# The gate of layer 0's attention sub-layer: its matrix-vector product moved from VectorE to column groups of TensorE

## The chip, the cores and the metric

The kernel runs on one core of a Trainium2 chip. The metric is device microseconds of one execution, lower is better. TensorE appears in the profile as PE (matmuls) and PEld (weight loads), VectorE as DVE, ScalarE as ACT, GpSimd as POOL, and the queue that issues the transfers as SP.

## What is computed

Two layers of an encoder trunk on 256 tokens of width 2048. In each layer a conditioning vector `c` gives six vectors of 2048 numbers (shift, scale and gate, for the attention sub-layer and for the feed-forward one). Each of the six is a product of a vector with a 2048 x 2048 matrix.

```python
cond = jax.nn.silu(c)
for l in range(DEPTH):
    mod = cond @ w_ada[l] + b_ada[l]
    sh1, sc1, g1, sh2, sc2, g2 = [m[:, None, :] for m in jnp.split(mod, 6, axis=-1)]
    u = x * (1.0 + sc1) + sh1
    proj = u @ w_in[l]
    ...
    y = jnp.concatenate([rms_norm(ya, ...), rms_norm(yb, ...), rms_norm(yc, ...)], axis=-1)
    x = layer_norm(DEEPNORM_ALPHA * x + (1.0 + g1) * (y @ w_o[l]), ln1_g[l], ln1_b[l])
    u = x * (1.0 + sc2) + sh2
    gu = u @ w_gu[l]
    h = jax.nn.silu(gu[..., :D_FF]) * gu[..., D_FF:]
    x = layer_norm(DEEPNORM_ALPHA * x + (1.0 + g2) * (h @ w_down[l]), ln2_g[l], ln2_b[l])
```

`ya`, `yb` and `yc` are three groups of attention heads (4, 6 and 6 heads) on slices of `proj`. The change is about `g1` of layer 0, which is needed for the first time at the output projection `y @ w_o[0]`.

## The kernel before

All data lie transposed: features on the 128 partitions, tokens along the free axis. Every weight matrix streams from HBM once, as pieces of 128 x 2048 fp32 (1 MB), through four buffers with the tag `raw` (`RAWB = 4`). For the large products a piece is split into two parts, `hi` (ACT, rounded) and `lo` (DVE, the rest), and TensorE multiplies these in its fast fp32r form; in layer 0 three matmuls of 256 columns stand for each 128 x 128 block (L289 to L291). Attention scores, the transposition of the probabilities (`ptp`), the product with V (`y`) and the small statistics (`st`) are plain fp32 matmuls.

The six modulation vectors are called parts 0 to 5: 0 and 1 are shift and scale of the attention, 2 is its gate, 4 and 3 scale and shift of the feed-forward, 5 its gate. Each part is 16 pieces of `w_ada`, which pass through the same four `raw` buffers. A piece holds, on its partitions, 128 outputs with all 2048 inputs along the free axis. One DVE instruction (L205, `tensor_tensor_reduce`) multiplies the piece with `cond`, copied to all partitions, and sums along the free axis to one column of `mods[l, part]`; a second tiny one writes the sum out. So there are 192 such instructions in the kernel.

They are dealt out in a fixed order by `pace`, which takes so many pieces off the list `ada_pending` per weight load or attention head; `need` takes what is left before a part is used. Parts 0 and 1 of layer 0 come at the very start, then the 16 pieces of part 2, then parts 4 and 3. Part 2's pieces run beside the stretch in which layer 0's input projection ends, group a's heads run, the latent projections (`in_22`, `in_20`, `in_21`, `in_16` to `in_19`, then `kn`, `vb`, `qn`, `qp`) are made, and group b's heads begin. A list scheduler orders the instructions on each engine by priority and readiness; pieces of part 2 have priority -1000, which puts them behind other work that is ready. On the chip each engine then goes through its list strictly in that order.

PSUM accumulators for the projections come from four banks of tag `g`; the transposed probabilities `pt` of the heads lie in two SBUF buffers of tag `pts`.

Of the kernel before, what the change touches and what calls it, by code (L numbers as in the profile page):

```python
# [10 lines left out]
F32 = mybir.dt.float32  # L11
F32R = mybir.dt.float32r
AF = mybir.ActivationFunctionType
ALU = mybir.AluOpType
# [3 lines left out]
P = 128  # L18
D = 2048
S = 256  # L20
L = 2
KT = D // P
# [11 lines left out]
ALPHA = (2 * L) ** 0.25  # L34
# [52 lines left out]
T2K, T1K, RAWB, HIB = 28, 24, 4, 4  # L87
# [2 lines left out]
RATE = ((0.19, 0.135, 0.135), (0.04, 0.05, 0.05))  # L90
NPOOL = 4


V_ADA, V_LN1G, V_LN1B, V_LN2G, V_LN2B = 0, 96, 112, 128, 144
V_QN, V_KVN, V_GN = 160, 164, 166

C_ID, C_FOLD, C_CS, C_MASK, C_ONES, C_DIST = 0, 128, 256, 512, 576, 704
NCONST = 1088
SLOPES = [float(np.float32(2.0 ** (-8.0 * (i + 1) / C_HEADS))) for i in range(C_HEADS)]


@with_exitstack
def tile_encoder(ctx: ExitStack, tc: tile.TileContext, xT, cB, w_ada, vecs, rpb, sink, consts,
                 w_in, w_va, w_vc, w_uq, w_ukv, w_o, w_gu, w_dn, out):
    nc = tc.nc
    pe, ve, ac, po, sy = nc.tensor, nc.vector, nc.scalar, nc.gpsimd, nc.sync

    cst = ctx.enter_context(tc.tile_pool(name="cst", bufs=1))
    wp = ctx.enter_context(tc.tile_pool(name="wp", bufs=1))
    sb = ctx.enter_context(tc.tile_pool(name="sb", bufs=1))  # L110
# [24 lines left out]
    cs = cst.tile([P, NCONST], F32, name="cs")  # L135
# [3 lines left out]
    maskc = cs[:, C_MASK:C_MASK + GRID_W]  # L139
    ones = cs[:, C_ONES:C_ONES + P]  # L140
    dist = cs[:, C_DIST:C_DIST + 384]
    cond = cst.tile([P, D], F32, name="cond")
    crow = wp.tile([P, D], F32, tag="raw", bufs=RAWB, name="crow")
    sy.dma_start(out=crow[:1], in_=cB)
    vec = cst.tile([P, L * NVEC], F32, name="vec")
    sy.dma_start(out=vec, in_=vecs)
    snk = cst.tile([P, L * C_HEADS], F32, name="snk")
    nsnk = cst.tile([P, L * C_HEADS], F32, name="nsnk")

# [7 lines left out]
    for i in range(0, D, 512):  # L157
        cb = pg(f"cond{i}")
        pe.matmul(cb[:], lhsT=one[:1, :P], rhs=crow[:1, i:i + 512], start=True, stop=True)
        ac.activation(out=cond[:, i:i + 512], in_=cb[:], func=AF.Silu)  # L160
    xspin = cst.tile([P, 512], F32R, name="xspin")
    ac.activation(out=xspin, in_=cond[:, :512], func=AF.Copy)
    eps_ln = cst.tile([P, 1], F32, name="eps_ln")
# [10 lines left out]
    mods = {}  # L174
# [14 lines left out]
    def ada_finish(l, part, c0, n):  # L189

        m = mods[l, part][:, c0:c0 + n]
        if part in (2, 5):
            ve.tensor_scalar(out=m, in0=m, scalar1=1.0, scalar2=1.0 / ALPHA, op0=ALU.add, op1=ALU.mult)
        elif part in (1, 4):
            ac.activation(out=m, in_=m, func=AF.Copy, bias=1.0)

    def ada(n):
        for _ in range(n):
            if not ada_pending:
                return  # L200
            l, part, k = ada_pending.pop(0)
            w = wp.tile([P, D], F32, tag="raw", bufs=RAWB, name=f"ada{l}_{part}_{k}")
            sy.dma_start(out=w, in_=w_ada[l, part * KT + k])
            with after(gate[0]), tc.high_priority(100 if l == 0 and part < 2 else -1000):
                ve.tensor_tensor_reduce(out=w, in0=w, in1=cond, op0=ALU.mult, op1=ALU.add, scale=1.0,  # L205
                                        scalar=vcol(l, V_ADA + part * KT + k), accum_out=mods[l, part][:, k:k + 1])
            g = ada_group(l, part)
            if k % g == g - 1:
                ada_finish(l, part, k + 1 - g, g)

    credit = [0.0, 0.0]

# [386 lines left out]
    for l in range(L):  # L599
# [103 lines left out]
        for h in range(A_HEADS):  # L703
            nv = nba[:, h].rearrange("p (r c) -> p r c", c=GRID_W)
            ve.scalar_tensor_tensor(out=nv, in0=nv, scalar=-1.0,
                                    in1=maskc.unsqueeze(1).to_broadcast([P, 6, GRID_W]),
                                    op0=ALU.mult, op1=ALU.add)
# [44 lines left out]
        for h in range(B_HEADS):  # L752
            acc = pg(f"kn{l}_{h}")
# [6 lines left out]
        for h in range(2):  # L760
            for j in range(2):
                acc = pg(f"vb{l}_{h}_{j}")
# [10 lines left out]
        for g in range(3):  # L773
            get = wload(w_uq[l, g], 2048, (1024, 1024))
            for j in range(2):
                h = 2 * g + j
                acc = pg(f"qn{l}_{h}")
# [3 lines left out]
                acc = pg(f"qp{l}_{h}")  # L781
# [35 lines left out]
        for n in range(KT):  # L817
# [5 lines left out]
            acc = pg(f"o{l}_{n}")  # L823
# [33 lines left out]
        for g in range(FFG):  # L857
            credit[1] = RATE[l][1 if g == 0 else 2]
            H = []
            for j in range(GSZ):  # L860
                f = g * GSZ + j
                hs = []
                for w in range(2):
# [5 lines left out]
                    if 2 * f + w < HB and l:  # L869
                        acc = head[2 * f + w]  # L870
                    else:
                        get = wload(w_gu[l, 2 * f + w], 2048, (1024, 1024))
                        acc = pg(f"gu{l}_{f}_{w}")
# [11 lines left out]
                if g == FFG - 1:  # L885
                    for n in range(2 * j, min(2 * j + 2, KT)):
                        need(l, 5, KT - 1 if l else n)
                        ve.scalar_tensor_tensor(out=ax[:, n], in0=mix[n], scalar=mods[l, 5][:, n:n + 1],
                                                in1=ax[:, n], op0=ALU.mult, op1=ALU.add)
            c1 = (GSZ + 1) // 2  # L890
            credit[1] = RATE[l][2]
            for n in range(KT):
# [8 lines left out]
                acc = pg(f"dn{l}_{g}_{n}")  # L901
# [32 lines left out]
def _pack(inp):  # L934
    f = {k: np.asarray(v) for k, v in inp.items()}
    a = {}
    a["xT"] = np.ascontiguousarray(f["x"][0].T.reshape(KT, P, S).transpose(1, 0, 2))
    a["cB"] = np.ascontiguousarray(f["c"].reshape(1, D))
    a["w_ada"] = np.ascontiguousarray(f["w_ada"].transpose(0, 2, 1)).reshape(L, 96, P, D)
    vecs = []  # L940
    for l in range(L):
# [15 lines left out]
    con = np.zeros((P, NCONST), np.float32)  # L957
# [10 lines left out]
    con[:, C_MASK:C_MASK + GRID_W] = np.tile(np.where(inside, 0.0, BIG), (2, 1))  # L968
    con[:, C_ONES:C_ONES + P] = 1.0
    dist = np.abs(np.arange(P)[:, None] - (np.arange(384)[None, :] - P)).astype(np.float32)  # L970
    con[:, C_DIST:C_DIST + 384] = np.where(dist <= P, dist, np.float32(1e34))
    a["consts"] = con

# [35 lines left out]
    for nm, ls in (("w_in", w_in), ("w_va", w_va), ("w_vc", w_vc), ("w_uq", w_uq), ("w_ukv", w_ukv),  # L1009
# [2 lines left out]
    return a  # L1012


_ORDER = ["xT", "cB", "w_ada", "vecs", "rpb", "sink", "consts", "w_in", "w_va", "w_vc", "w_uq",
          "w_ukv", "w_o", "w_gu", "w_dn"]


# [17 lines left out]
```

## Time and profile before

| quantity | value |
|---|---|
| median of 3 runs | 2336.89 us (2335.63 to 2347.25) |
| profiled execution, its own time | 2353.45 us |
| its span in the trace | 2351.7 us |
| mean granted TensorE clock | 0.984 |
| instructions of L205 (modulation pieces on DVE) | 192, 16 of them part 2 of layer 0 |

Times in the rows are microseconds from the start of the span. A matmul's row is one record; records overlap, because a record includes the time in which results drain, so the distance from one start to the next tells what a matmul costs in a full stream.

### The profile page before, as it was taken

What the parts mean: (1) busy time and instruction counts of PE and PEld (TensorE: products, weight loads), DVE (VectorE), ACT (ScalarE), POOL (GpSimd) and SP (SyncE); (2) the same over time, 40 slices, a digit from 0 to 9 for tenths busy, and PEclk for the clock granted to TensorE, in tenths of its full rate; (3) what the DMA queues carried; (4) which work ended last, traced back from release to release, by engine and by line L of the source; (5) the groups of instructions that cost most, each with busy time, mean ns of one, the idle gap of its engine ahead of it and who ended that gap; (6) DMA issues with size and microseconds to landing.
All of it is one profiled execution on the core that took longest, in us unless ns stands there. A gap on an engine that the chain in (4) does not pass through costs nothing.

```text
span 2351.7 us, 34259 instructions
## 1 busy us (share of the span) xinstructions
PE 2244.0 (95%) x13286; PEld 1973.5 (84%) x13286; DVE 1763.9 (75%) x2498; ACT 1209.2 (51%) x2054; POOL 200.5 (9%) x175
## 2 busy tenths in 40 slices
PE   5789999999999999999999999999999999999997
PEld 4678899898788888888877888888888888888886
DVE  7789888798788788898877676778666666556556
ACT  3446654564444444444547665657444444444445
POOL 0000010000000200110140000330000011011014
PEclk9989999999999999999999999999999999999999
DMA  9997887588888799788755445455567666546543
GB/s 370 352 350 293 295 331 280 185 327 291 294 325 311 272 334 322 274 324 332 278 207 198 170 179 198 151 208 213 213 236 255 235 205 231 184 160 216 179 159 110
DMA packets 88438, 590.72 MB, mean 251 GB/s; under 512 B 9937, under 2 KB 10065, under 8 KB 28881
## 3 DMA queue, kind: packets, MB, share of 16 engines
q1 hardware_dynamic: 88274, 588.52, 69.5%
q8 instruction: 104, 1.70, 0.3%
q14 instruction: 60, 0.49, 0.1%
HBM read 586.39 MB, written 2.10 MB: 250 GB/s over the span
## 4 chain that ended last, share of the span: by engine, by line
PE 69%; issue 18%; DVE 7%; ACT 3%; POOL 1%; DMA 1%; ACTq 0%; POOLq 0%; DVEq 0%; SPq 0%
PE gu L268 18%; PE gu L269 9%; PE dn L268 8%; PE dn L269 4%; PE o L279 4%; DVE ada L205 3%; PE in L268 3%; DVE lo L253 2%; PE o L268 2%; ACT hi L252 2%; PE in L269 1%; PE in L289 1%; PE in L291 1%; PE in L290 1%; PE o L269 1%
## 5 line engine op out<-in xcount | busy, mean ns | idle before, releaser
L253 DVE TENSOR_TENSOR lo<-raw,hi 128x1024 fp32r<-128x1024 f32 (+2 forms) x808 | 904.1, 1130 | 369.8 <-ACT hi L252 365.8
L252 ACT ACTIVATE hi<-raw 128x1024 fp32r<-128x1024 f32 (+2 forms) x808 | 776.7, 970 | 700.7 <-PE gu L268 244.7
L268 PE MATMUL gu<-X,hi 128*128 128x512 f32 x2528 | 892.8, 398 | 0.0
L269 PE MATMUL gu<-X,lo 128*128 128x256 f32 x2528 | 710.8, 281 | 5.0 <-DVE lo L253 4.8
L268 PEld LDWEIGHTS gu<-X,hi 128*128 128x128 f32 x2528 | 475.5, 188 | 116.6
L205 DVE CUSTOM_DVE_ANT_0 ada<-ada,cond,vec 128x2048 f32<-128x2048 f32 x192 | 449.7, 2350 | 55.8 <-DMA ada<-in_w_ada 46.5
L268 PE MATMUL dn<-H,hi 128*128 128x512 f32 x1386 | 489.3, 398 | 1.2 <-DVE H L315 1.2
L269 PEld LDWEIGHTS gu<-X,lo 128*128 128x128 f32 x2528 | 478.3, 189 | 5.9 <-DVE lo L253 5.9
L269 PE MATMUL dn<-H,lo 128*128 128x256 f32 x1386 | 389.0, 282 | 11.6 <-DVE lo L253 11.6
L268 PEld LDWEIGHTS dn<-H,hi 128*128 128x128 f32 x1386 | 260.2, 188 | 64.9 <-DVE H L315 2.8
L269 PEld LDWEIGHTS dn<-H,lo 128*128 128x128 f32 x1386 | 261.7, 189 | 16.3 <-DVE lo L253 16.0
L310 POOL TENSOR_TENSOR mix<-mix,cma 128x256 f32<-128x256 f32 x64 | 78.5, 1227 | 1185.5 <-ACT cma L309 1176.9
L289 PE MATMUL in<-X,hi 128*128 128x256 f32 x368 | 106.2, 313 | 41.9 <-ACT X L314 35.3
L289 PEld LDWEIGHTS in<-X,hi 128*128 128x128 f32 x368 | 73.3, 212 | 47.2 <-ACT X L314 39.1
L290 PE MATMUL in<-X,hi 128*128 128x256 f32 x368 | 110.2, 303 | 1.5 <-DVE X L315 1.5
L291 PE MATMUL in<-X,lo 128*128 128x256 f32 x368 | 107.6, 302 | 1.8 <-DVE lo L253 1.8
L268 PE MATMUL in<-X,hi 128*128 128x512 f32 x272 | 97.0, 398 | 0.0
L880 ACT ACTIVATE gu<-gu 128x256 f32<-128x256 f32 x82 | 34.2, 418 | 94.3 <-DVE gu L305 94.3
L290 PEld LDWEIGHTS in<-X,hi 128*128 128x128 f32 x368 | 76.9, 209 | 2.7 <-DVE X L315 2.1
L291 PEld LDWEIGHTS in<-X,lo 128*128 128x128 f32 x368 | 75.4, 208 | 3.0 <-DVE lo L253 2.6
L269 PE MATMUL in<-X,lo 128*128 128x256 f32 x272 | 77.9, 286 | 0.0
L305 DVE SCALAR_TENSOR_TENSOR gu<-gu,cmb 128x256 f32<-128x256 f32 x158 | 65.9, 417 | 3.3 <-ACT cmb L302 3.2
(351 smaller groups left out, 2906.6 us busy)
## 6 DMA issues: line engine op xcount, KB each, us to landing
ada<-in_w_ada SPq DMA_DIRECT2D x192, 1024.0 KB, 6.0
raw<-in_w_gu SPq DMA_DIRECT2D x176, 1024.0 KB, 5.3
raw<-in_w_dn SPq DMA_DIRECT2D x128, 704.0 KB, 4.2
raw<-in_w_in SPq DMA_DIRECT2D x46, 1024.0 KB, 4.8
raw<-in_w_o SPq DMA_DIRECT2D x32, 1024.0 KB, 5.0
raw<-in_w_va SPq DMA_DIRECT2D x8, 1024.0 KB, 4.8
raw<-in_w_uq SPq DMA_DIRECT2D x6, 1024.0 KB, 4.7
raw<-in_w_vc SPq DMA_DIRECT2D x4, 1024.0 KB, 6.8
```

The costliest lines, as they stand in the source:

```text
L205: ve.tensor_tensor_reduce(out=w, in0=w, in1=cond, op0=ALU.mult, op1=ALU.add, scale=1.0, scalar=vcol(l, V_ADA + part * KT + k), accum_out=m ...
L252: ac.activation(out=hi[:, :n], in_=raw[:, c0:c0 + n], func=AF.Copy)
L253: eng.tensor_tensor(out=lo[:, :n], in0=raw[:, c0:c0 + n], in1=hi[:, :n].bitcast(F32), op=ALU.subtract)
L268: pe.matmul(acc[:], lhsT=h, rhs=X[k][:], start=(i == 0), stop=False)
L269: last_mm[0] = raw_ins(pe.matmul(acc[:, :S], lhsT=lo, rhs=X[k][:, :S], start=False, stop=(i == len(kts) - 1)))
L279: m_ = pe.matmul(acc[:, :S], lhsT=w, rhs=x, start=(i == 0), stop=(i == len(ops) - 1))
L289: pe.matmul(acc[:, :S], lhsT=h, rhs=x[:, :S], start=first, stop=False)
L290: pe.matmul(acc[:, :S], lhsT=h, rhs=x[:, S:], start=False, stop=False)
L291: last_mm[0] = raw_ins(pe.matmul(acc[:, :S], lhsT=lo, rhs=x[:, :S], start=False, stop=end))
L305: ve.scalar_tensor_tensor(out=dst, in0=acc[:, :S], scalar=scale, in1=t, op0=ALU.mult, op1=ALU.add)
L310: po.tensor_tensor(out=dst, in0=dst, in1=t, op=ALU.add)
L880: ac.activation(out=hs[0], in_=hs[0], func=AF.Silu)
```

## The change

Part 2 of layer 0 is taken off DVE. Its 16 MB arrive as a second array `w_adag`, 16 pieces of the same size in the same places of the list, but laid out with inputs on the partitions: piece (g, i) holds 512 outputs (group g of 4) for four blocks of 128 inputs (4i to 4i+3). `conds` holds `silu(c)` with inputs on partitions, each of the 16 columns repeated 32 times. For each piece TensorE runs four fp32 matmuls of 512 columns (L234), with 32 stationary columns each, one for each block of inputs, placed in the four column groups 0, 32, 64 and 96 of the array; they add into one PSUM bank `arow` whose four groups of 32 partitions hold four partial sums. After four pieces ACT copies the bank to SBUF (`arsb`, from the tag `pts`), four fp32 matmuls with one column (`sel`, L242) add the four partial sums and turn the row into four columns, and DVE adds the bias and scales. The input of the three others is unchanged: all other parts stay on DVE.

```diff
+PE_ADA = ((0, 2),)
+    condT = cst.tile([P, KT], F32, name="condT")
+    sy.dma_start(out=condT, in_=cT)
+    conds = cst.tile([P, KT, 32], F32, name="conds")
...
+    ac.activation(out=condT, in_=condT, func=AF.Silu)
+    ve.tensor_copy(out=conds, in_=condT.unsqueeze(2).to_broadcast([P, KT, 32]))
...
             l, part, k = ada_pending.pop(0)
+            if (l, part) in PE_ADA:
+                ada_pe(l, part, k // 4, k % 4)
+                continue
...
+    def ada_pe(l, part, g, i):
+
+        w = wp.tile([P, D], F32, tag="raw", bufs=RAWB, name=f"adap{l}_{part}_{g}_{i}")
+        sy.dma_start(out=w, in_=w_adag[PE_ADA.index((l, part)), g, i])
+        if i == 0:
+            rows[0] = pg(f"arow{l}_{part}_{g}")
+        acc = rows[0]
+        first = None
+        for j in range(4):
+            with after(first), tc.high_priority(1000 if j else -1000):
+                m_ = pe.matmul(acc[32 * j:32 * j + 32, :], lhsT=conds[:, 4 * i + j], rhs=w[:, j * 512:(j + 1) * 512],
+                               start=(i == 0), stop=(i == 3), tile_position=(0, 32 * j))
+            first = first or raw_ins(m_)
+        if i == 3:
+            with tc.high_priority(-1000):
+                r = sb.tile([P, 512], F32, tag="pts", bufs=2, name=f"arsb{l}_{part}_{g}")
+                ac.activation(out=r, in_=acc, func=AF.Copy)
+                for c in range(4):
+                    pe.matmul(acc[:, c:c + 1], lhsT=r[:, c * P:(c + 1) * P], rhs=sel, start=True, stop=True)
+                m = mods[l, part][:, 4 * g:4 * g + 4]
+                plus = 1.0 if part in (1, 2, 4, 5) else 0.0
+                ve.scalar_tensor_tensor(out=m, in0=acc[:, 0:4], scalar=plus, in1=vcol(l, V_ADA + part * KT + 4 * g, 4),
+                                        op0=ALU.add, op1=ALU.add)
+                if part in (2, 5):
+                    ve.tensor_scalar(out=m, in0=m, scalar1=1.0 / ALPHA, scalar2=None, op0=ALU.mult)
```

The change makes the scheduler deal the instructions out anew in this stretch. In the rows below the last number of a name is a buffer number; `arow_2_0` is group 0 of part 2, `adap_2_0_2` its piece 2, and "x4" stands for four matmuls in a row. Line numbers of the changed kernel are 39 higher from the helpers for weights on.

On PE, behind the last products of group a's values (`va`), there stood the work of group a's heads and of the projection `in_22`:

```order
L637 MATMUL va_1_2_1197<-hi_1_1244,X_15_1006 128x512
L385 MATMUL ptp_a_1_1324<-dg_a_1_1316,pp_a_1_1315 128x128
L289 MATMUL in_22_8_1428<-X_9_591,hi_1_1163 128x256
L290 MATMUL in_22_8_1428<-X_9_591,hi_1_1163 128x256
L291 MATMUL in_22_8_1428<-X_9_591,lo_1_1164 128x256
```

and now three pieces in a row stand ahead of that work:

```order
L676 MATMUL va_1_2_1206<-hi_1_1259,X_15_1011 128x512
L234 MATMUL arow_2_0_1161<-adap_2_0_2_1247,conds 32x512 x4
L234 MATMUL arow_2_0_1161<-adap_2_0_3_1291,conds 32x512 x4
L234 MATMUL arow_2_1_1334<-adap_2_1_0_1332,conds 32x512 x4
L328 MATMUL in_22_8_1460<-X_8_536,hi_1_1172 128x256
L329 MATMUL in_22_8_1460<-X_8_536,hi_1_1172 128x256
L429 MATMUL ya_0_1290<-pt_a_0_1324,Va_0_707 128x256
```

The 16 pieces stand at nine places of PE's list: five alone, one pair and three rows of three. On DVE, where the query projections end and group b's heads begin (`qp` is a query, `mn_b_0` the row minimum of head 0's scores), there stood

```order
L784 TENSOR_TENSOR qp_4_2005<-qp_4_2005,cs 128x256
L205 ISA ada_2_14_2116,mod_2_99<-ada_2_14_2116,cond,vec 128x2048
L205 ISA mod_2_99 128x1
L205 ISA ada_2_15_2181,mod_2_99<-ada_2_15_2181,cond,vec 128x2048
L784 TENSOR_TENSOR qp_5_2036<-qp_5_2036,cs 128x256
L365 TENSOR_REDUCE mn_b_0_2061<-s_b_0_2056 128x1
L193 TENSOR_SCALAR mod_2_99<-mod_2_99 128x4
L205 ISA ada_4_0_2216,mod_4_101<-ada_4_0_2216,cond,vec 128x2048
```

and now head 0 of group b follows the second query directly:

```order
L823 TENSOR_TENSOR qp_0_1909<-qp_0_1909,cs 128x256
L823 TENSOR_TENSOR qp_1_1940<-qp_1_1940,cs 128x256
L404 TENSOR_REDUCE mn_b_0_2133<-s_b_0_2128 128x1
L292 TENSOR_TENSOR lo_0_1972<-raw_1969,hi_0_1971 128x1024
L292 TENSOR_TENSOR lo_1_1976<-raw_1969,hi_1_1975 128x1024
L404 TENSOR_REDUCE mn_b_0_2133<-s_b_0_2128 128x1
L418 RECIPROCAL rs_b_0_2134<-rs_b_0_2134 128x2
```

The pieces that left DVE stand among those heads on PE; here is the second row of three, with the four one-column matmuls of a finished group behind it:

```order
L831 MATMUL s_b_3_2225<-kpe_1489,qp_3_2026 128x256
L234 MATMUL arow_2_2_1665<-adap_2_2_2_1877,conds 32x512 x4
L234 MATMUL arow_2_2_1665<-adap_2_2_3_1955,conds 32x512 x4
L234 MATMUL arow_2_3_2043<-adap_2_3_0_2041,conds 32x512 x4
L242 MATMUL arow_2_2_1665<-cs,arsb_2_2_1961 128x1 x4
L429 MATMUL yb_0_2121<-pt_b_0_2149,vb_1844 128x256 x2
L424 MATMUL ptp_b_1_2173<-dg_b_1_2165,pp_b_1_2164 128x128 x2
```

From the last quarter of layer 0's output projection on, the order on every engine is as before.

## Rows read from the trace of the kernel before

**Rows 1.** The page: span, busy time of each engine, DMA share in 40 slices.

```profile
span 2351.7 us, 34259 instructions
PE 2244.0 (95%) x13286; PEld 1973.5 (84%) x13286; DVE 1763.9 (75%) x2498; ACT 1209.2 (51%) x2054; POOL 200.5 (9%) x175
...
DMA  9997887588888799788755445455567666546543
```

**Rows 2.** Stretches around part 2: busy time of each engine, clock, DMA.

```profile
core 0: us, PE busy (x) PEld busy (x) DVE busy (x) ACT busy (x) POOL busy (x), PEclk, DMA share, GB/s
145.00:170.00 25.00, 24.15 (x163) 22.14 (x162) 22.56 (x45) 14.11 (x26) 0.00 (x0) 1.00 0.79 294
170.00:195.00 25.00, 23.84 (x154) 21.10 (x153) 22.82 (x39) 13.38 (x27) 0.00 (x0) 1.00 0.84 321
195.00:220.00 25.00, 21.85 (x165) 21.02 (x163) 24.19 (x45) 16.51 (x33) 0.00 (x0) 1.00 0.76 277
220.00:245.00 25.00, 21.82 (x153) 21.05 (x154) 23.86 (x31) 10.52 (x23) 0.00 (x0) 0.91 0.89 342
245.00:270.00 25.00, 25.00 (x144) 22.63 (x144) 20.69 (x39) 17.84 (x45) 0.00 (x0) 0.89 0.74 271
```

**Rows 3.** The instructions of L205: duration min/median/max, ns; first and last start.

```profile
L205 DVE CUSTOM_DVE_ANT_0 ada<-ada,cond,vec x192: 2329/2345/2932, 10.4 to 1946.3; 128x2048 f32<-128x2048 f32 x192
L205 DVE DVE_READ_ACCUMULATOR2_ANT mod<- x192: 74/81/86, 12.7 to 1948.6; 128x1 f32 x192
```

**Rows 4.** Waits from 130 to 260 us: total, times, longest.

```profile
PE s_b L791 <- ACT pp_b L373: 3.1, 1, 3.1
...
PE qn L291 <- DVE lo L253: 1.4, 1, 1.4
...
PE qn L289 <- ACT Xq L314: 1.2, 1, 1.2
```

**Rows 5.** DVE in order of time where group b's heads begin.

```profile
235.96 2.35 DVE L205 CUSTOM_DVE_ANT_0 ada<-ada,cond,vec 128x2048 f32<-128x2048 f32 x1
...
238.23 2.35 DVE L205 CUSTOM_DVE_ANT_0 ada<-ada,cond,vec 128x2048 f32<-128x2048 f32 x1
...
240.84 0.41 DVE L365 TENSOR_REDUCE mn_b<-s_b 128x1 f32<-128x256 f32 x1
...
241.24 2.34 DVE L205 CUSTOM_DVE_ANT_0 ada<-ada,cond,vec 128x2048 f32<-128x2048 f32 x1
```

**Rows 6.** Pieces of the chain that ended last: start, duration, what.

```profile
198.30 0.34 PE st_kv L322 x4
...
220.90 0.21 PE qn L290
...
223.77 0.12 PE qp L289
...
248.36 1.71 PE ptp_b L385 x8
...
251.67 0.86 PE yb L390 x4
252.53 0.89 PE ptp_b L385 x8
```

**Rows 7.** The fp32 matmuls of L390 for group b, both layers.

```profile
L390 PE MATMUL yb<-pt_b,vb x48: 379/379/483, 251.5 to 1414.4; 128*128 128x256 f32 x48
```

**Rows 8.** PE in order of time: an fp32 matmul between fp32r ones.

```profile
178.03 0.60 PE L390 MATMUL ya<-pt_a,Va 128*128 128x256 f32 x2
178.28 0.47 PE L291 MATMUL in<-X,lo 128*128 128x256 f32 x1
178.58 0.28 PE L289 MATMUL in<-X,hi 128*128 128x256 f32 x1
```

**Rows 9.** DMA at the start, and a load's median time to landing.

```profile
1.12 0.36 SPq L146 DMA_DIRECT2D vec<-in_vecs  x1
...
ada<-in_w_ada SPq DMA_DIRECT2D x192, 1024.0 KB, 6.0
```

More of the change, by code (lines that the diff above doesn't have):

```diff
@@ L91, with tile_encoder @@
 NPOOL = 4
+PE_ADA = ((0, 2),)
 V_ADA, V_LN1G, V_LN1B, V_LN2G, V_LN2B = 0, 96, 112, 128, 144
 V_QN, V_KVN, V_GN = 160, 164, 166
-C_ID, C_FOLD, C_CS, C_MASK, C_ONES, C_DIST = 0, 128, 256, 512, 576, 704
-NCONST = 1088
+C_ID, C_FOLD, C_CS, C_MASK, C_ONES, C_DIST, C_SEL = 0, 128, 256, 512, 576, 704, 1088
+NCONST = 1090
 SLOPES = [float(np.float32(2.0 ** (-8.0 * (i + 1) / C_HEADS))) for i in range(C_HEADS)]
 @with_exitstack
-def tile_encoder(ctx: ExitStack, tc: tile.TileContext, xT, cB, w_ada, vecs, rpb, sink, consts,
+def tile_encoder(ctx: ExitStack, tc: tile.TileContext, xT, cB, cT, w_ada, w_adag, vecs, rpb, sink, consts,
                  w_in, w_va, w_vc, w_uq, w_ukv, w_o, w_gu, w_dn, out):
@@ L141, in tile_encoder @@
     dist = cs[:, C_DIST:C_DIST + 384]
+    sel = cs[:, C_SEL:C_SEL + 1]
     cond = cst.tile([P, D], F32, name="cond")
@@ L209, in ada @@
                 ada_finish(l, part, k + 1 - g, g)
+    rows = {}
+    def ada_pe(l, part, g, i):
[22 more added lines that the diff above has]
+                    ve.tensor_scalar(out=m, in0=m, scalar1=1.0 / ALPHA, scalar2=None, op0=ALU.mult)
     credit = [0.0, 0.0]
@@ L938, in _pack @@
     a["cB"] = np.ascontiguousarray(f["c"].reshape(1, D))
+    a["cT"] = np.ascontiguousarray(f["c"].reshape(KT, P).T)
+    a["w_adag"] = np.stack([f["w_ada"][l][:, p * D:(p + 1) * D].reshape(4, 4, P, 4, 512).transpose(3, 0, 2, 1, 4)
+                            for l, p in PE_ADA]).reshape(len(PE_ADA), 4, 4, P, D)
     a["w_ada"] = np.ascontiguousarray(f["w_ada"].transpose(0, 2, 1)).reshape(L, 96, P, D)
@@ L970, in _pack @@
     dist = np.abs(np.arange(P)[:, None] - (np.arange(384)[None, :] - P)).astype(np.float32)
+    con[::32, C_SEL] = 1.0
     con[:, C_DIST:C_DIST + 384] = np.where(dist <= P, dist, np.float32(1e34))
@@ L1012, in _pack @@
     return a
-_ORDER = ["xT", "cB", "w_ada", "vecs", "rpb", "sink", "consts", "w_in", "w_va", "w_vc", "w_uq",
+_ORDER = ["xT", "cB", "cT", "w_ada", "w_adag", "vecs", "rpb", "sink", "consts", "w_in", "w_va", "w_vc", "w_uq",
           "w_ukv", "w_o", "w_gu", "w_dn"]
```

## The prediction

> **What bounds the kernel now.** The page comes first [rows 1]: TensorE is busy for 95% of the span, VectorE for 75%. That average mixes stages, so the next view is the table of stretches [rows 2]. The 16 pieces of part 2 lie in its first 100 us, the last of them at 238.23 [rows 5]. There VectorE looks like the limit: 22.56, 22.82, 24.19 and 23.86 busy out of 25, together 93.4 of 100 us. But TensorE is busy for 24.15 + 23.84 + 21.85 + 21.82 = 91.7 of the same 100, so at most 8.3 us of it are free. The transfers are at 0.76 to 0.89. Three resources stand close together here, and the question is which of them others wait for. The list of waits answers it [rows 4]: TensorE waited for something that VectorE or ScalarE made 3.1, 1.4 and 1.2 us, 5.7 in all. The longest of these is seen in VectorE's order of time [rows 5]: two pieces (235.96 and 238.23), 2.35 us each, stand ahead of the first row minimum of group b's scores at 240.84, and another one at 241.24 ahead of the next; the exponential waits for the minimum, and the scores of later heads wait for the exponential. After such a pause the clock is lower: the granted clock is 0.91 from 220 to 245 and 0.89 from 245 to 270 [rows 2], that is (0.09 + 0.11) x 25 / 0.5 = 10 us at 1.2 instead of 2.4 GHz. A 256-column record then takes 0.21 us (at 220.90) instead of 0.12 (at 223.77), and eight records of `ptp` 1.71 instead of 0.89 [rows 6]. So VectorE is crowded, but TensorE sets the end, and it has little room.
>
> **What goes.** Sixteen times a multiply-and-sum of 2.345 us and a read-out of 0.081 [rows 3]: 16 x 2.43 = 38.8 us of VectorE. What that is worth is not 38.8 us but what TensorE had to wait for, and what the low clock after it cost. The most is 8.3 us of idle time plus 5 us (half of the 10 at 1.2 GHz), 13.3. The least is the two waits directly behind pieces or behind work that they pushed back, 3.1 + 1.4, and some of the clock, about 6. I take 10, since waits for weights, for statistics and for results of the neighbours remain. Faster VectorE work triggers earlier splits of weights and so earlier loads; with the transfers at 0.82 on average this helps nothing while TensorE has the work queued already.
>
> **What comes on TensorE.** No row shows a matmul in a quarter of the array, so its price is bounded. An fp32 matmul appears as two records: the 24 products with V of group b (six heads, two each, two layers) are 48 records [rows 7]. Four such records of 256 columns take 0.86 us in a full stream [rows 6], so a record of 512 columns takes 0.43, and one fp32 matmul of 512 columns 0.86. A piece is four of them.
>
> - Lower bound: the four column groups run fully side by side, and a piece takes 0.86 us; 16 pieces 13.8.
> - Upper bound: one after the other, 3.44 us a piece; 55.0.
> - Between: the second record of a matmul uses the same columns as the first, so it must wait for it; if records also begin in the order of the list, the next group's first record can only begin beside the previous group's second. Then a piece alone takes five record times (2.15 us) and n pieces in a row 4n + 1. The 16 pieces stand as five alone, one pair and three rows of three: 25 + 9 + 39 = 73 record times, 31.4 us.
>
> I take the third, 31.4, since it gives the columns their parallel work without letting records pass one another; the nearest row, two records per fp32 matmul one behind the other, leans this way. The Trainium skill, "TensorE: Matmul & The Clock Gate", section "Part 3: Packing small matmuls — row/col tiling", says that matmuls in different column groups overlap, and that matmuls start and end strictly in program order. No row of this kernel shows either.
>
> The 16 one-column matmuls that turn the sums (32 records) cost what the statistics cost: four records in 0.34 us [rows 6], so 32 x 0.085 = 2.7. A change of form on TensorE is not free: between an fp32 matmul and the next fp32r one, the record that begins at 178.28 holds the stream for 0.30 us [rows 8] instead of 0.12, 0.18 more. Nine places make 1.6; if it is paid on entry and exit, 3.2. The Trainium skill, "TensorEngine Tiling (Array Packing)", section "Key Properties", says that a change of tiling mode drains the engine, a rule against dealing out the pieces singly; the 0.18 is the nearest that this trace has for it.
>
> Small things: one more transfer stands on the queue ahead of the first weights, 0.36 us like its neighbour [rows 9], in a start whose transfers are at 0.9 and more [rows 1]: +0.4. The four ScalarE copies and eight short VectorE instructions fall on engines with room. Every load stays in its place of the queue, but its buffer is now freed by TensorE instead of VectorE. Where pieces are queued far down TensorE's list they hold buffers: the last query weights can only be requested when the piece ahead of group b's fourth score is done. A load takes 6.0 us to land [rows 9]; behind it stand four fp32 score matmuls of 256 columns (1.7 us) and three pieces (5.6), which cover it. If pieces take only 0.86, that cover shrinks to 4.3, and about 2 us show.
>
> **The sum.** 31.4 + 2.7 + 1.6 + 0.4 = 36.1 added to TensorE's path, less 10 given back: +26. Against the profiled execution (2353.45 us, span 2351.7) this is 2379.6; that execution lies 16.6 above the median of the runs shown, 2336.89, to which I add it: 2363 us, 1.1% slower. What can be told from no change in a measurement of this kernel is about 0.5%, 12 us.
>
> **Rivals.**
>
> *Side by side.* All four columns stream at once, 0.86 us a piece: 13.8 + 4.7 - 10 = +8.5, 2345 us, which is not slower by what can be told. For it: four instructions of a piece stand directly behind one another, into disjoint columns. Against it: each is two records. It decides where a piece costs less than about (12 + 10 - 4.7) / 16 = 1.1 us. With all 13.3 given back it is +5, 2342. The Trainium skill, "TensorE: Matmul & The Clock Gate", section "Part 3: Packing small matmuls — row/col tiling", gives a measured speedup of 2.38 for three column groups of 512 columns; by an estimate from that figure alone a piece would take 3.44 / 2.38 = 1.4 us. No row here shows it.
>
> *One after another.* The columns don't overlap in fp32: 55.0 + 4.7 - 10 = +50, 2387 us. For it: every fp32 record in this trace begins where the previous one's stream ends [rows 6].
>
> *VectorE is the bound after all.* Its 93.4 of 100 us set the pace through the buffers that it frees, and the stretch shrinks until the transfers fill it: at 0.82 on average 100 us become 82, -18, 2319 us. Against it: TensorE's 91.7 us plus at least 18.5 don't fit into 82. It would need most of the busy time on TensorE to be drain that overlaps.
>
> **How the numbers follow.** Pairs (the sum) 0.42, side by side 0.32, one after another 0.22, VectorE the bound 0.04. Slower by over 0.5%: 0.40 from the pairs (they fall below +12 only with far more given back), 0.22, and a quarter of the side-by-side case, 0.08: 0.70. Within 0.5%: the rest of these two, 0.26. Faster: 0.04. The range goes from side by side with everything given back and a few small waits less (2340) to one after another with little given back (2390: 55.0 + 4.7 - 6 = +54). The likeliest case alone, with 6 to 13 given back and switches on one or both sides, is 2360 to 2369.
>
> **What would show it.** In the changed kernel's trace the time from one piece's first record to the next piece's first, in a row of three, is 0.9 (side by side), 1.7 (pairs) or 3.4 us (one after another). VectorE's busy time in the stretch falls by about 39 us. The wait of 3.1 us ahead of group b's scores goes, and the granted clock there is 1.00. Layer 0's output projection starts later by about the change in the whole time, and from there on the two traces run in step; a difference that arises behind it would make the argument wrong, and so would a pause of TensorE at a piece whose load has not landed.

## The result, and the profile after

The changed kernel takes 2355.44 us (median of 8 runs, 2350.62 to 2359.66) beside 2339.21 for the kernel before (8 runs, 2333.86 to 2347.64) on the same chip: a ratio of 1.006, 95% interval 1.0038 to 1.0081, so 14 us longer by the ratio, 9 to 19 by its interval. The forecast was 2363, within 2340 to 2390. Its direction and range held. The price of its largest term was twice too high, the time given back was right in size but had another cause, and the cost of held buffers was left out of the sum.

The page of the changed kernel, the lines that answer to [rows 1]:

```profile
span 2357.9 us, 34547 instructions
PE 2256.8 (96%) x13446; PEld 1976.1 (84%) x13446; DVE 1733.5 (74%) x2471; ACT 1211.0 (51%) x2059; POOL 202.6 (9%) x175
```

TensorE has 160 more records (128 of the pieces, 32 of one column) and 12.8 us more busy time; VectorE has 30 us less over the whole span. The stretches, which answer to [rows 2]:

```profile
core 0: us, PE busy (x) PEld busy (x) DVE busy (x) ACT busy (x) POOL busy (x), PEclk, DMA share, GB/s
145.00:170.00 25.00, 24.48 (x171) 20.80 (x170) 16.63 (x39) 13.51 (x25) 0.00 (x0) 1.00 0.71 262
170.00:195.00 25.00, 24.98 (x161) 20.16 (x160) 8.43 (x20) 11.16 (x24) 0.00 (x0) 1.00 0.64 239
195.00:220.00 25.00, 24.83 (x204) 21.27 (x202) 17.72 (x39) 13.71 (x27) 0.00 (x0) 1.00 0.80 278
220.00:245.00 25.00, 25.00 (x173) 22.90 (x172) 13.09 (x28) 15.37 (x38) 0.00 (x0) 1.00 0.37 126
245.00:270.00 25.00, 25.00 (x181) 19.02 (x180) 11.23 (x27) 14.68 (x37) 0.00 (x0) 1.00 0.69 272
270.00:295.00 25.00, 20.70 (x145) 19.33 (x144) 21.44 (x33) 13.16 (x22) 0.00 (x0) 0.93 0.84 334
```

From 145 to 245 VectorE's busy time falls from 93.4 to 16.63 + 8.43 + 17.72 + 13.09 = 55.9 us, 37.6 less, as worked out beforehand (38.8). TensorE's idle time there falls from 8.3 to 0.7 us: the 3.1 us ahead of group b's scores are gone, and the granted clock from 220 to 270 is 1.00 instead of 0.91 and 0.89. But a new hole stands at 270 to 295: 4.3 us idle, clock 0.93.

What a piece costs is read from TensorE's order of time. The columns are start, duration, line, names, form, count of records; the distance to the next start is the cost:

```profile
159.56 1.06 PE L234 MATMUL arow<-adap,conds 128*32 128x512 f32 x8
160.56 0.38 PE L328 MATMUL in<-X,hi 128*128 128x256 f32 x1
...
176.65 2.78 PE L234 MATMUL arow<-adap,conds 128*32 128x512 f32 x24
179.36 0.38 PE L328 MATMUL in<-X,hi 128*128 128x256 f32 x1
...
196.66 0.95 PE L242 MATMUL arow<-cs,arsb 128*128 128x1 f32 x8
197.54 1.06 PE L234 MATMUL arow<-adap,conds 128*32 128x512 f32 x8
...
198.97 1.92 PE L234 MATMUL arow<-adap,conds 128*32 128x512 f32 x16
200.82 0.39 PE L328 MATMUL in<-X,hi 128*128 128x256 f32 x1
...
242.52 1.06 PE L234 MATMUL arow<-adap,conds 128*32 128x512 f32 x8
243.51 0.70 PE L830 MATMUL s_b<-kn,qn 128*128 128x256 f32 x2
```

A row of three pieces takes 179.36 - 176.65 = 2.71 us, 0.90 each with the change of form in it; the pair takes 1.85, a piece alone 1.00 and 0.99. That is the "side by side" case of the forecast, whose taken value for three in a row was 13 record times, 5.6 us. The weight loads of the same row of three show how the four column groups run:

```profile
176.65 0.16 PEld L234 LDWEIGHTS arow<-adap,conds 128*32 128x32 f32 x8 [0.35 <-issue]
177.10 0.13 PEld L234 LDWEIGHTS arow<-adap,conds 128*32 128x32 f32 x4 [0.30 <-issue]
177.53 0.13 PEld L234 LDWEIGHTS arow<-adap,conds 128*32 128x32 f32 x4 [0.30 <-issue]
```

They come in fours, 0.43 us apart. Among TensorE's single records the first four of a piece start at 176.649, .655, .662 and .669, the next four at 177.102 to 177.122. A record doesn't name its column group; but records in one column group start 0.43 us apart (run 3 below), so four that start within 20 ns must be of four groups: first records of all four groups, then second records of all four. The Trainium skill, "TensorE: Matmul & The Clock Gate", section "Part 3: Packing small matmuls — row/col tiling", models a packed group as the time of one matmul and about 4 ns for each further one; the trace has that form, with 6 to 7 ns in place of 4. Its figure for three groups, a speedup of 2.38, would by the forecast's estimate make a piece 1.4 us; the trace has 0.86 to 0.90.

The new hole lies behind group b's heads (in brackets the idle time ahead of the row, and who ended it):

```profile
272.17 1.13 PE L429 MATMUL yb<-pt_b,vb 128*128 128x256 f32 x4 [0.69 <-ACT pt_b L427]
...
274.72 0.39 PE L328 MATMUL in<-X,hi 128*128 128x256 f32 x1 [1.42 <-ACT hi L291]
...
275.98 0.39 PE L330 MATMUL in<-X,lo 128*128 128x256 f32 x1 [0.76 <-DVE lo L292]
...
288.09 0.39 PE L328 MATMUL in<-X,hi 128*128 128x256 f32 x1 [0.87 <-ACT hi L291]
...
289.17 0.39 PE L330 MATMUL in<-X,lo 128*128 128x256 f32 x1 [0.57 <-DVE lo L292]
```

TensorE waits there for the splits of group c's weights, because these were asked for late. The transfers' queue in order of time:

```profile
243.64 0.33 SPq L283 DMA_DIRECT2D raw<-in_w_uq  x1
246.56 2.04 SPq L227 DMA_DIRECT2D adap<-in_w_adag  x3
251.98 12.61 SPq L214 DMA_DIRECT2D ada<-in_w_ada  x2
266.03 0.33 SPq L283 DMA_DIRECT2D raw<-in_w_in  x1
```

The last three pieces on TensorE, and the first of group c's weights in the trace before:

```profile
264.91 2.78 PE L234 MATMUL arow<-adap,conds 128*32 128x512 f32 x24
```

```profile
238.34 0.33 SPq L244 DMA_DIRECT2D raw<-in_w_in  x1
```

Three of the four buffers are taken by the last three pieces from 246.56 on, and these stand in one row of three on TensorE, at 264.91. The fourth buffer alone serves the next two pieces, one of part 4 and one of part 3, one after the other. So the first of group c's weights is asked for at 266.03; in the trace before it was at 238.34. The end of it all is the first record of the layer norm behind the output projection:

```profile
448.44 0.62 PE L464 MATMUL spina<-xspin 128*128 128x512 f32 x2
```

It was at 435.68 before, so 12.8 us later.

### The profile page after: what moved, and what is told of

Same layout as the page of the kernel before. It is cut to its first block, busy times and chain, and to the rows that moved or that the text cites. A ratio compares the mean times of both kernels' runs of the same rounds, so it can differ in the third digit from the quotient of the medians.

```text
span 2357.9 us, 34547 instructions
## 1 busy us (share of the span) xinstructions
PE 2256.8 (96%) x13446; PEld 1976.1 (84%) x13446; DVE 1733.5 (74%) x2471; ACT 1211.0 (51%) x2059; POOL 202.6 (9%) x175
## 4 chain that ended last, share of the span: by engine, by line
PE 70%; issue 18%; DVE 7%; ACT 3%; DMA 2%; POOL 1%; ACTq 0%; POOLq 0%; DVEq 0%
PE gu L307 18%; PE gu L308 9%; PE dn L307 8%; PE o L318 4%; PE dn L308 4%; PE in L307 3%; DVE ada L216 2%; PE o L307 2%; DVE lo L292 2%; DMA ada<-in_w_ada 2%; ACT hi L291 1%; PE in L308 1%; PE in L328 1%; PE in L330 1%; PE in L329 1%
## 5 line engine op out<-in xcount | busy, mean ns | idle before, releaser
L216 DVE CUSTOM_DVE_ANT_0 ada<-ada,cond,vec 128x2048 f32<-128x2048 f32 x176 | 412.4, 2351 | 46.2 <-DMA ada<-in_w_ada 39.8
L308 PEld LDWEIGHTS dn<-H,lo 128*128 128x128 f32 x1386 | 261.7, 189 | 13.3 <-DVE lo L292 12.8
L845 POOL TENSOR_SCALAR nbc<-cs 128x384 f32<-128x384 f32 x12 | 19.4, 1614 | 590.1 <-DVE mn_c L411 439.2
```

Of the source, the lines that this page charges most:

```text
L308: last_mm[0] = raw_ins(pe.matmul(acc[:, :S], lhsT=lo, rhs=X[k][:, :S], start=False, stop=(i == len(kts) - 1)))
L845: po.tensor_scalar(out=nb, in0=dist, scalar1=SLOPES[h], scalar2=None, op0=ALU.mult)
```

## The experiments

Eleven runs were made, two of them of the unchanged programs. Times are against runs of the kernel before on the same chip, in us at its median of 2339 to 2346. The last columns are from one profile each: from group a's first scores (150.03 in the trace before) to the layer norm's first record (435.68), the stretch that holds all that the change touches behind the kernel's start, and its difference to 285.5, the mean of two profiles of the kernel before.

| kernel | time against before | stretch, us | difference |
|---|---|---|---|
| before, two profiles | | 285.6, 285.4 | |
| changed, two profiles | +14.0 (+9 to +19), +13.8 (+9 to +19) | 298.3, 300.3 | +12.8, +14.8 |
| 1: relief alone | -3.0 (-6.6 to +0.5) | 283.9 | -1.6 |
| 2: pieces early | +13.4 (+8 to +18) | 294.9 | +9.4 |
| 3: one column group | +56.0 (+49 to +63) | 336.1 | +50.6 |
| 4: pieces twice | +25.8 (+20 to +31) | 306.2 | +20.7 |
| 6: TensorE's work alone | +12.7 (+8 to +17) | 294.8 | +9.2 |
| 7: both, no buffer held | +8.4 (+4 to +13) | 294.7 | +9.2 |
| 8: relief and no loads | -13.8 (-19 to -9) | 274.1 | -11.4 |
| 10: rate 0.165 | -2.8 (-6 to +1) | 285.3 | -0.2 |
| 11: rate 0.145 | +0.2 (-3 to +4) | 285.6 | +0.1 |

**1. Relief alone.** What is VectorE's relief worth by itself?

```diff
-                ve.tensor_tensor_reduce(out=w, in0=w, in1=cond, ...)
+                if (l, part) == (0, 2):
+                    ve.tensor_copy(out=mods[l, part][:, k:k + 1], in_=w[:, k:k + 1])
+                else:
+                    ve.tensor_tensor_reduce(out=w, in0=w, in1=cond, ...)
```

> The kernel before, with the 16 sums of part 2 left out: each piece is still loaded, and VectorE only copies one of its columns, which frees the buffer (the gate of layer 0 is then not computed). Theory: TensorE sets the pace, and without any work added to it the waits of 3.1 and 1.4 us and the low clock from 220 to 250 us go: 8 to 13 us faster than before (2326 to 2331). Rival (VectorE's relief is worth next to nothing): 0 to 5 us faster. Rival (VectorE was the bound of the stretch): 18 us faster or more.

It is 3.0 us faster (2340.89, 12 runs; ratio 0.9987, interval 0.9972 to 1.0002), which can't be told from nothing. The theory of 8 to 13 fell; the rival of 0 to 5 holds. Two stretches of its trace, and two waits in them:

```profile
170.00:195.00 25.00, 20.92 (x112) 17.99 (x111) 12.52 (x28) 11.43 (x22) 0.00 (x0) 0.86 0.66 259
...
220.00:245.00 25.00, 22.41 (x165) 21.08 (x165) 14.52 (x28) 11.90 (x27) 0.00 (x0) 1.00 0.98 380
```

```profile
189.10 0.58 PE L294 MATMUL in<-X,lo 128*128 128x256 f32 x1 [2.46 <-DVE lo L256]
...
241.63 0.70 PE L794 MATMUL s_b<-kn,qn 128*128 128x256 f32 x2 [1.99 <-ACT pp_b L376]
```

VectorE has 10 us and more to spare in each stretch, and TensorE still idles 4.1 and 2.6 us. The 2.46 us ahead of split weights are new. The 1.99 us are what is left of the 3.1 us of [rows 4]: the same wait for group b's exponential. VectorE's order of time shows why it stayed:

```profile
237.95 0.42 DVE L368 TENSOR_REDUCE mn_b<-s_b 128x1 f32<-128x256 f32 x1 [0.88 <-PE s_b L795]
238.29 2.34 DVE L208 CUSTOM_DVE_ANT_0 ada<-ada,cond,vec 128x2048 f32<-128x2048 f32 x1
...
240.56 0.75 DVE L368 TENSOR_REDUCE mn_b<-s_b 128x1 f32<-128x256 f32 x2
```

A piece of the next part, which the change leaves on VectorE, stands between the first row minimum and the next two. It is the one that stood at 241.24 in [rows 5]. The transfers are at 0.98 in the second stretch.

**2. Pieces early.** Is the hole behind group b's heads what the change costs? All four matmuls of a piece get priority 1000, so that the last pieces come before group b's later heads.

```diff
-            with after(first), tc.high_priority(1000 if j else -1000):
+            with after(first), tc.high_priority(1000):
```

> The changed kernel with the first matmul of each piece at priority 1000 instead of -1000, so that a piece is put on TensorE's list as soon as its load is due; the last four pieces then stand 90 rows earlier and the weights of group c's keys can be asked for earlier. Theory (buffers held by pieces far down the list cost about 7 us, at 271 to 289 us): 5 to 9 us slower than before instead of 14, and no pause of TensorE behind group b's heads. Rival (the 14 us are TensorE's added work alone): 13 to 16 us slower than before.

The hole is gone:

```profile
270.00:295.00 25.00, 24.97 (x191) 23.90 (x191) 18.37 (x34) 15.97 (x34) 0.00 (x0) 1.00 0.68 247
```

The time says +13.4, the rival's side; the stretch says +9.4, 3.4 to 5.4 less than in the changed kernel. The first of group c's weights is asked for at 242.54, instead of 266.03. At an interval of 10 us the time alone can't decide between 9 and 14, and the stretch became readable only with runs 5 and 9, which show how far it scatters.

**3. One column group.** All four matmuls of a piece go to columns 0 to 31, one after another.

```diff
-                m_ = pe.matmul(acc[32 * j:32 * j + 32, :], lhsT=..., rhs=...,
-                               start=(i == 0), stop=(i == 3), tile_position=(0, 32 * j))
+                m_ = pe.matmul(acc[0:32, :], lhsT=..., rhs=...,
+                               start=(i == 0 and j == 0), stop=(i == 3 and j == 3), tile_position=(0, 0))
...
```

The copy and the one-column matmuls then take 32 partitions instead of 128.

> The changed kernel with all four matmuls of a piece in column group 0, summed in the same 32 partitions. Theory (TensorE's time is paid in full, a piece goes from 0.86 to 3.44 us): 41 us more than the changed kernel, 50 to 58 us slower than before. Rival (TensorE has room behind waits, which takes a part of it): 25 to 40 us slower than before. The trace tells the price of a piece by the distance of its records: 0.43 between all eight, instead of four at once.

It is 56 us slower (2398.47, 4 runs; ratio 1.0239, interval 1.0211 to 1.0267), as the theory had it. Four pieces stand in a row on TensorE. The first 26 of their 32 records, those that begin ahead of 190.00, take 11.35 us, less 0.16 for the last one's drain 0.43 each:

```profile
178.87 11.35 PE L234 MATMUL arow<-adap,conds 128*32 128x512 f32 x26
```

Eight records make a piece, 3.44 us: the forecast's upper bound, exactly. Four column groups are worth a factor of 3.44 / 0.86 = 4.0 here. Behind group b's heads, from 270 to 295, TensorE idles only 0.05 us in this run, so it has no hole there to compare with that of the changed kernel.

**4. Pieces twice.** Each piece's four matmuls are issued twice, and `sel` is halved.

```diff
-        for j in range(4):
+        for t in range(8):
+            j = t % 4
...
```

> The changed kernel with the four matmuls of each piece issued twice, and the selecting column halved, so that the sums stay right. Theory (a piece costs 0.86 us of TensorE, all of it on the path): 13.8 us more than the changed kernel, 26 to 30 us slower than before. Rival (pieces are partly hidden in waits for weights): 14 to 22 us slower than before.

25.8 us slower (2368.28, 4 runs; ratio 1.011, interval 1.0086 to 1.0134), just below the theory's 26 to 30. Four doubled pieces stand in a row, 64 records in 7.00 us, 0.875 for eight:

```profile
175.92 7.08 PE L235 MATMUL arow<-adap,conds 128*32 128x512 f32 x64
182.92 1.13 PE L430 MATMUL ya<-pt_a,Va 128*128 128x256 f32 x4
```

The hole from 270 to 295 is smaller here as well (1.15 us of idle time). So runs 3 and 4 are best set beside the kernels without the hole (294.7 to 294.9 in runs 2, 6 and 7): run 3's stretch is 41.3 us longer, for 16 x 2.58 = 41.3 us of added work, run 4's 11.4 for 16 x 0.875 = 14.0. Once its gaps are filled, TensorE's time counts in full or nearly. Beside the changed kernel itself run 4's stretch grows by only 6 to 8 us, since less of the hole is left.

**5. The kernel before once more.** The same program, for a second profile.

> The kernel before once more, for a second profile of it: how far does the place where layer 0's attention ends (first row of the first layer norm, 435.68 in the first profile) differ between two executions of one program? If stretches are comparable to a few tenths, it lies at 435 to 436; if single profiles scatter as the times do (2334 to 2351), it can lie anywhere from 430 to 440.

The layer norm's first record is at 435.83 instead of 435.68, and the stretch is 285.4 instead of 285.6. What comes behind differs much more: from there to TensorE's last record 1904.7 us in the first profile and 1888.0 in the second, over the same instructions. So stretches can be compared far better than spans of single profiles: to a few tenths here, to 2.0 us in the two profiles of the changed kernel (run 9).

**6. TensorE's work alone.** VectorE keeps its passes; TensorE runs the same 64 column-group matmuls, copies and one-column matmuls on a table that lies in SBUF anyway. Only the short add at the end is a copy.

```diff
+            if (l, part) in PE_ADA:
+                ada_pe(l, part, k // 4, k % 4)
...
-                m_ = pe.matmul(acc[32 * j:32 * j + 32, :], lhsT=conds[:, 4 * i + j], rhs=w[:, j * 512:(j + 1) * 512],
+                m_ = pe.matmul(acc[32 * j:32 * j + 32, :], lhsT=conds[:, 4 * i + j], rhs=cond[:, j * 512:(j + 1) * 512],
```

> The pieces' work on TensorE alone, without the relief: VectorE keeps its 16 passes of part 2 and the gate comes from them; in addition TensorE runs the same 64 matmuls in four column groups, at the places where pieces are dealt out, but over a constant table (cond, already in SBUF) in place of the loaded pieces, with the copies and the one-column matmuls, whose result nobody uses. No buffer is held by TensorE. Theory (TensorE's added time is paid in full, 14 to 15 of pieces, 2.7 of one-column matmuls, about 2 of switches): 17 to 20 us above the kernel before. Rival (TensorE's 8 us of idle time and low clock in the stretch swallow part of it): 6 to 12 above. Rival that held buffers cost most in the changed kernel: under 8.

12.7 us slower (2354.57, 9 runs; ratio 1.0054, interval 1.0036 to 1.0071), 9.2 in the stretch: not the theory's 17 to 20, and by the stretch the first rival's 6 to 12: TensorE's own gaps swallow half of its new work. Its stretches:

```profile
170.00:195.00 25.00, 25.00 (x170) 19.88 (x163) 21.87 (x32) 13.14 (x26) 0.00 (x0) 1.00 0.81 312
195.00:220.00 25.00, 25.00 (x207) 19.90 (x209) 21.75 (x42) 11.95 (x25) 0.00 (x0) 1.00 0.63 228
220.00:245.00 25.00, 24.86 (x182) 22.55 (x175) 23.27 (x36) 14.24 (x29) 0.00 (x0) 1.00 0.86 336
245.00:270.00 25.00, 25.00 (x171) 23.16 (x170) 24.37 (x47) 18.52 (x49) 0.00 (x0) 1.00 0.90 325
```

VectorE is as busy as before, 21.8 to 24.4 of 25, and TensorE has hardly a gap and full clock. The waits of [rows 4] are gone with nothing taken off VectorE: while TensorE works on pieces, what it would have waited for gets done. These pieces wait for no load, and the scheduler puts some of them elsewhere, the last three at 288.16 instead of 264.91.

**7. Both, with no buffer held.** The changed kernel over the same table; each loaded piece is freed by a one-column copy on VectorE.

```diff
+        with tc.high_priority(-1000):
+            ve.tensor_copy(out=mods[l, part][:, 4 * g + i:4 * g + i + 1], in_=w[:, i:i + 1])
...
-                m_ = pe.matmul(..., rhs=w[:, j * 512:(j + 1) * 512],
+                m_ = pe.matmul(..., rhs=cond[:, j * 512:(j + 1) * 512],
```

> The changed kernel with its pieces' matmuls over the constant table cond in place of the loaded piece (so the gate is not computed), and each loaded piece freed by a copy of one column on VectorE: the same matmuls, VectorE relieved as in the changed kernel, and no buffer waits for TensorE. Theory (TensorE's time in full, relief worth about 3): 13 to 17 above the kernel before, the same as the changed kernel. Rival (buffers held by queued pieces cost 5 or more): 9 or less above.

8.4 us slower (2352.86, 11 runs; ratio 1.0036, interval 1.0019 to 1.0054), 9.2 in the stretch, the same as runs 2 and 6 (294.7 to 294.9 in all three). Against run 6 only VectorE's 16 passes are gone, and the stretch doesn't change. Against the changed kernel the held buffers are gone, and the stretch is 3.6 to 5.6 shorter; the first of group c's weights is asked for at 238.46 (242.16 in run 6). The last three pieces stand at 288.97 here, so a part of the difference could be their place; but run 2, which keeps the loaded pieces and puts them early, has the same stretch. By the time this falls to the rival (9 or less), though its interval touches the theory's 13.

**8. Relief and no loads.** As run 1, and part 2's 16 pieces are not loaded either.

```diff
-            w = wp.tile([P, D], F32, tag="raw", bufs=RAWB, name=f"ada{l}_{part}_{k}")
-            sy.dma_start(out=w, in_=w_ada[l, part * KT + k])
+            if (l, part) != (0, 2):
+                w = wp.tile([P, D], F32, tag="raw", bufs=RAWB, name=f"ada{l}_{part}_{k}")
+                sy.dma_start(out=w, in_=w_ada[l, part * KT + k])
```

> The kernel before without part 2's sums and without its 16 loads (the gate of layer 0's attention is left out): VectorE has 38.8 us less, and 16 MB less pass through the four buffers. Theory (the relief alone was worth only 3 because loads and the four buffers were next to be late): the idle time and the low clock of the stretch go, 10 to 13 us below the kernel before. Rival (what was late next is a chain of statistics and results, not loads): 2 to 5 below, as without the sums alone.

13.8 us faster (2329.87, 6 runs; ratio 0.9941, interval 0.992 to 0.9962), 11.4 in the stretch, the theory's side. Without the loads TensorE has hardly a gap from 170 to 245:

```profile
170.00:195.00 25.00, 24.82 (x176) 23.00 (x176) 16.12 (x45) 17.95 (x42) 0.00 (x0) 1.00 0.23 75
195.00:220.00 25.00, 24.95 (x193) 24.58 (x193) 20.31 (x37) 16.79 (x34) 0.00 (x0) 1.00 0.62 214
220.00:245.00 25.00, 25.00 (x174) 23.34 (x173) 22.64 (x34) 15.27 (x35) 0.00 (x0) 1.00 0.88 334
```

Taking off the sums gives 1.6 us of the stretch, taking off the loads as well 11.4. But the order on VectorE changes too. Where group b's heads begin, the next two row minima (234.36) now follow the first (232.90) after one split of weights of 1.22 us, and no modulation piece stands between them. So the gaps that run 1 left go with the 16 loads; whether by the buffers, by the transfers or by the order of the other engines isn't shown. A kernel without the loads that keeps the sums was not run.

**9. The changed kernel once more.**

> The changed kernel once more, beside the others on one chip. Theory (TensorE's added 19 us less about 10 of its own gaps that the new work fills, plus about 4 for buffers held by queued pieces): layer 0's attention ends 12 to 13.5 us later than in the kernel before (448.4 in the first profile, 435.7 and 435.8 in the two profiles of before), and the time is 10 to 16 above. Rival (the 4 us between the changed kernel and the ones without the pause are scatter): the attention ends 8 to 11 later.

13.8 us slower (2360.16, 7 runs; ratio 1.0059, interval 1.0037 to 1.0081). The layer norm begins at 452.50, 16.8 later than in the trace before, more than the theory's 13.5; 2.1 of that had already arisen ahead of group a's scores, and the stretch itself is 300.3. The hole is there again, with 0.69, 1.42, 0.75, 0.87 and 0.58 us, and the clock behind it is lower than in the first profile, 0.86 instead of 0.93:

```profile
270.00:295.00 25.00, 20.69 (x132) 19.09 (x129) 17.82 (x32) 13.20 (x22) 0.00 (x0) 0.86 0.80 307
```

That is 0.07 x 25 = 1.8 us of full clock, nearly all of the 2.0 us between the two profiles. Against 294.8 without the hole, the stretches put the cost of the held buffers at 3.5 and 5.5 us. The times don't resolve it: +14.0 and +13.8 with the hole, +13.4, +12.7 and +8.4 without, each with an interval of 8 us or more.

**10 and 11. Fewer loads in the stretch.** If loads are late, it might pay to deal them out later. The kernel before, with one number changed:

```diff
-RATE = ((0.19, 0.135, 0.135), (0.04, 0.05, 0.05))
+RATE = ((0.165, 0.135, 0.135), (0.04, 0.05, 0.05))
```

> The kernel before with its own VectorE passes, but with the modulation pieces of layer 0's attention dealt out at a rate of 0.165 instead of 0.19 for each microsecond of work: some three or four loads fewer stand ahead of group b's heads, and they come in the output projection, where transfers are at 0.75. Theory (in this stretch a load fewer is worth 12.5/16 = 0.8 us, since loads and buffers are what is late there): 2 to 4 us below the kernel before, at the end of the attention and in the time. Rival (what is taken off here is late in the output projection): 0, or some us above.

and with 0.145:

> As the run at 0.165, with a rate of 0.145: six or seven loads fewer ahead of group b's heads. Theory: 4 to 6 us below. Rival: 0, or 5 and more above, since a row of eight pieces then stands ahead of the last output weights.

Neither can be told from the kernel before (ratios 0.9988, interval 0.9973 to 1.0003, and 1.0001, interval 0.9986 to 1.0016). At 0.145 group c's products with V end 17 us earlier than before (332.4 instead of 349.3), and all of it is lost in the output projection, where the loads now stand. The list of waits from 355 to 440 has one long entry for TensorE, and the last stretch shows it idle and at a low clock:

```profile
PE o L279 <- ACT hi L252: 12.1, 1, 12.1
```

```profile
370.00:440.00 70.00, 57.32 (x446) 55.80 (x445) 57.21 (x82) 21.81 (x32) 0.00 (x0) 0.90 0.79 300
```

The rival was right. No version here beats the kernel before while it does all of the work.

## Why the prediction was right, and where it was wrong

**The sum, term by term.**

| term | forecast | measured |
|---|---|---|
| 16 pieces with their switches | 31.4 + 1.6 | 5 x 1.0 + 1.85 + 3 x 2.71 = 15.0 |
| one-column matmuls | 2.7 | 0.88 + 0.88 + 0.91 + 0.85 = 3.5 |
| start | 0.4 | 0.1 (group a's scores at 150.12 instead of 150.03; 2.2 in the second profile, not in the sum) |
| given back | -10 | -9.3 (18.5 less the 9.2 of runs 6 and 7) |
| buffers held by queued pieces | 0 | +3.5 to +5.5 |
| sum | +26 | +12.8 to +14.8; timed +14 |

The one-column matmuls stand in four places, at 196.66, 207.30, 248.15 and 268.62. The pieces, the one-column matmuls and the start are measured by themselves. The two terms below them are differences of stretches, so the sum has to come out at the changed kernel's stretch and is no check on them.

**The failed step** is "if records also begin in the order of the list, the next group's first record can only begin beside the previous group's second". In the trace all four groups' first records begin within 20 ns, and their second ones 0.43 us behind: 0.86 us a piece and not 2.15. Runs 3 and 4 confirm the price from both sides: 3.44 us with one column group, 0.875 for each four groups added. The rival "side by side" had the piece right, and its +8.5 is near what the stretch gained wherever the hole was gone (+9.2, +9.2, +9.4).

**Given back: right in size, wrong in cause.** The 10 us were put down to the 38.8 us that leave VectorE. Run 1 takes these away alone and gains 1.6 us in the stretch, 3.0 timed. Run 6 leaves them and adds TensorE's work, and the stretch grows by 9.2 where 18.5 were added; run 7 does both and also grows by 9.2. So the relief is worth nothing measurable in the stretch beside the pieces: their own time fills TensorE's gaps. The windows from 145 to 440, summed over the kernel before:

```profile
sum 295.00, PE 282.93 PEld 268.52 DVE 257.78 ACT 157.28 POOL 8.09; mean PE 282.93 PEld 268.52 DVE 257.78 ACT 157.28 POOL 8.09
```

and over run 6:

```profile
sum 295.00, PE 289.33 PEld 264.83 DVE 254.68 ACT 157.59 POOL 7.97; mean PE 289.33 PEld 264.83 DVE 254.68 ACT 157.59 POOL 7.97
```

TensorE's idle time falls by 6.4 us. The granted clock is below 1.00 in three windows of 25 us before (0.91, 0.89, and 0.93 from 345 to 370), a shortfall of 0.27 x 25 = 6.8 us, and in one of run 6 (0.86 from 345 to 370), 3.5: 3.3 less. Together that is about 9.7 of the 18.5, an estimate that counts every microsecond at the low clock as half lost. The two timings (12.7 and 8.4) leave open a relief of some us.

**What the gaps are made of.** The forecast's "5.7 in all" is the three longest waits; from 145 to 270 TensorE waits 8.2 us for VectorE and ScalarE, all but 0.1 of its idle time there. It put the low clock down to the wait ahead of group b's scores, but its own slow record at 220.90 [rows 6] lies ahead of that wait and behind those for `qn`. And it took the 3.1 us as given back with part 2. Two of the pieces in [rows 5] are part 2's, but the one at 241.24, ahead of the next row minima, is part 4's and stays on VectorE. With part 2's sums gone (run 1) 2.0 of the 3.1 us remained behind that piece, and a wait of 2.46 us for a split of weights came up. With TensorE's added work (run 6) or without the loads as well as the sums (run 8) the gaps closed. That wait ended with a split at 187.83, which stood on VectorE behind group a's closing work (from 184.80 on); its weights had landed at 177.13 and its `hi` was ready at 185.14. So both waits of run 1 end in the order of VectorE's list, and neither at a load that landed late. Why they go with the loads in run 8 stays open.

**The held buffers** were in the forecast as a sentence ("about 2 us show" if pieces take 0.86), and not in the sum. The mechanism was right: pieces far down TensorE's list hold buffers. The last query weights were asked for as it said, at 243.64, right behind the piece at 242.52; but they were being split at 248.51, and TensorE has no gap from 220 to 270. The cost came at a later load: group c's first weights, behind two pieces that had to share the one free buffer. By the stretches it was 3.5 to 5.5 us.

**What was right as put.** VectorE's busy time fell by 37.6 us (39 forecast). The wait of 3.1 went and the clock from 220 to 270 is 1.00. The output projection's end moved by 12.8 in the first profile and 16.8 in the second, beside a timed +14. "From there on the two traces run in step" can't be tested with one pair of profiles, since the part behind scatters by 17 us between two profiles of the kernel before. A pause at a piece whose load had not landed did not occur. "VectorE the bound" is refuted by run 1.

The total was too long by 12 us: 18 too much for pieces and switches (33.0 for 15.0), against about 4.5 for the buffers left out of the sum and 1 for the small terms. That the errors have opposite signs is luck, and so, in part, is the direction: at 0.86 us a piece the forecast's own terms give +8.5, which it called not slower by what can be told. The buffers, which it had left out, carried the time past that line.

## What to carry to other kernels

Where a busy engine has gaps, test them from both sides before paying for relief: take the suspected work away, and, separately, add the new work without the relief. Here the second gave 9.2 of the 12.8 to 14.8 us of the stretch, and the first showed that the relief was worth next to nothing. Four fp32 matmuls of 32 columns in four column groups were worth their full factor here (0.86 us for 3.44), so price them side by side; and when a consumer moves to another engine, ask at which place of that engine's list a load's buffer comes free, since a row of three consumers held three of four buffers for 18 us.

## What was not expected of the hardware

- An fp32 matmul of 512 columns appears as two records, and four such matmuls in four column groups run as two steps of 0.43 us, the four records of a step starting 6 to 7 ns apart. Whether they were listed in that order or passed one another, the trace doesn't say.
- One program's part behind the first attention, with nothing changed in it, took 1888.0 us in one profile and 1904.7 in another, while the stretch ahead of it agreed within 0.3 us (2.0 for the changed kernel).
